# Sixteen transposed products of 512x512: two PSUM banks per copy, no block, transposes between halves, and a small early write

## The chip, the cores and the metric

The kernel runs on one core of one Trainium2 chip. The metric is the device time of one execution in microseconds; lower is better. A profiled execution also gives a span, from the first to the last instruction of the core.

## The reference

```python
def setup_inputs():
    batch, m, k, n = 16, 512, 512, 512
    return {
        "a": np.random.randn(batch, k, m).astype(np.float32),
        "b": np.random.randn(batch, n, k).astype(np.float32),
    }

def reference(a, b):
    return np.matmul(a.transpose(0, 2, 1), b.transpose(0, 2, 1)).astype(np.float32)
```

Both inputs come transposed. TensorE wants the contracted axis k on the partitions for both operands: a has it there already, b has n there and must be turned first. Each of a, b and the output is 1 MB (1.049 million bytes) per batch, so an execution reads 33.55 MB and writes 16.78 MB.

## The kernel before

Each batch i goes through the same steps, spread over five engines that meet at semaphores. All waits are written out by hand inside one critical section (L42), and the engines' programs stand in a `Block` (L99): each engine branches into its own part at the start, and at the end of the block all engines meet at a barrier before the critical section ends with one of its own.

- SyncE issues all DMAs on one queue: the load of b (L108), the load of a (L111) and, five batches later (`LAG`), the store of a finished batch (L123). Each moves 128 rows of 8 KB. There are four input buffers for each of a and b (`LOADS`) and seven output buffers (`OUTS`). The load of b waits until the transposes of the batch four earlier are done (semaphore `turned`), the load of a until the first group of matmuls of that batch is done (`summed`). A store waits for `summed` to reach a later batch, which shows that the copies are over; the last two stores wait for the copies' own semaphores (L122).
- VectorE casts b to bfloat16 (`cast`, L145). TensorE transposes it as pairs of bfloat16 that are taken for one float32: eight transposes per batch (`transposes`, L78) into `bt_ps`. VectorE copies the result to SBUF (`turn`, L151).
- ScalarE casts a to bfloat16 (L183).
- TensorE does the product in four groups of four matmuls (`matmuls`, L90). Group rm fills one PSUM bank, `o_ps[rm]`, and counts up `summed`.
- VectorE copies the groups 0 and 2 out of PSUM (L167), ScalarE 1 and 3 (L194), one bank per copy. Each copy gives its bank back by a semaphore (`od_go` or `oa_go`), which TensorE takes before it fills the bank again.
- GpSimd builds the identity matrix for the transposes (L129, L131).

TensorE's order is: transposes of batch i+1, product of batch i, and so on; a loop of two batches per turn is followed by a tail:

```python
multiply(0, 0, steady)
turn(1)
pe.wait_ge(ac2_go, 1)
multiply(1, 1, last)
```

In this tail batch 14 is multiplied, batch 15 transposed and multiplied. There the cast of a is shared between ScalarE (first half) and VectorE (second half, L175, semaphore `ac2_go`).

Of the kernel before, what the change touches and what calls it, by code (L numbers as in the profile page):

```python
# [11 lines left out]
def kernel(  # L12
# [6 lines left out]
    nc = tc.nc  # L19
    P = 128  # L20
    B, K, M = a.shape
    _, N, _ = b.shape
    KO = K // P
    KJ = KO // 2
    MO = M // P
    NO = N // P
    assert B % 2 == 0

    f32 = mybir.dt.float32
    cdt = mybir.dt.bfloat16  # L30
# [3 lines left out]
    a_v = a.rearrange("b (ki ko) m -> b ki ko m", ko=KO)  # L34
    b_v = b.rearrange("b (ni no) k -> b ni no k", no=NO)
    out_v = out.rearrange("b (mi mo) n -> b mi mo n", mo=MO)

    LOADS = 4
    OUTS = 7
    LAG = 5  # L40

    with tc.tile_critical():  # L42
        sb = lambda name, shape, dt: ctx.enter_context(nc.sbuf_tensor(name, shape, dt))
        ps = lambda name, shape, dt: ctx.enter_context(nc.psum_tensor(name, shape, dt))
        sem = tc.alloc_semaphore
        a_sb = [sb(f"a_sb{s}", [P, KO, M], f32) for s in range(LOADS)]
        b_sb = [sb(f"b_sb{s}", [P, NO, K], f32) for s in range(LOADS)]
        o_sb = [sb(f"o_sb{s}", [P, MO, N], f32) for s in range(OUTS)]
        a_bf = [sb(f"a_bf{s}", [P, KO, M], cdt) for s in range(2)]
# [1 line left out]
        bt_sb = [sb(f"bt_sb{s}", [P, KJ, N], f32) for s in range(2)]  # L51
        identity = sb("identity", [P, P], f32)
        bt_ps = [ps(f"bt_ps{s}", [P, KJ, NO, P], f32) for s in range(2)]
        o_ps = [ps(f"o_ps{s}", [P, N], f32) for s in range(MO)]


        a_in = [sem(f"a_in{s}") for s in range(LOADS)]
# [2 lines left out]
        turned = sem("turned")  # L60
# [4 lines left out]
        bt_go = sem("bt_go")  # L65
        ac_go = sem("ac_go")
        ac2_go = sem("ac2_go")
        oa_go = sem("oa_go")
        od_go = sem("od_go")

        def transposes(pe, x, y):

            w = b_bf[x][:].bitcast(f32).rearrange("p no (pk j) -> p no j pk", j=KJ)
            for j in range(KJ):
                for no in range(NO):
                    last = pe.transpose(bt_ps[y][:, j, no, :], w[:, no, j, :], identity[:])  # L78
            last.then_inc(turned, 1)

        def take(pe, s):
            pe.wait_ge(s, 1).then_inc(s, -1)  # L82

        def matmuls(pe, x, y, waits):
            a_r = a_bf[x][:].rearrange("p rk (pm rm) -> p rk rm pm", rm=MO)
            bt_h = bt_sb[y][:].bitcast(cdt).rearrange("p j (n h) -> p j h n", h=2)
            for rm in range(MO):
                waits(rm)
                for rk in range(KO):
                    last = pe.matmul(  # L90
                        o_ps[rm][:],
                        a_r[:, rk, rm, :],
                        bt_h[:, rk // 2, rk % 2, :],
                        start=(rk == 0),
                        stop=(rk == KO - 1),
                    )
                last.then_inc(summed, 1)

        with nc.Block() as block:  # L99

            @block.sync
            def _(sp):
                for i in range(B + LAG):
                    s, use = i % LOADS, i // LOADS
                    if i < B:
                        if use:
                            sp.wait_ge(turned, i - LOADS + 1)
                        sp.dma_start(b_sb[s][:], b_v[i]).then_inc(b_in[s], 16)  # L108
                        if use:
                            sp.wait_ge(summed, MO * (i - LOADS) + 1)  # L110
                        sp.dma_start(a_sb[s][:], a_v[i]).then_inc(a_in[s], 16)  # L111
                    j = i - LAG
                    if j >= 0:


                        if j + 2 < B:
                            sp.wait_ge(summed, MO * (j + 2))
                        else:

                            sp.wait_ge(summed, MO * (B - 1))  # L120
                            for s in (oa_go, od_go):
                                sp.wait_ge(s, 2 * (j + 3 - B))  # L122
                        sp.dma_start(out_v[j], o_sb[j % OUTS][:]).then_inc(o_out[j % OUTS], 16)  # L123
                for s in range(OUTS):
                    sp.wait_ge(o_out[s], 16 * len(range(s, B, OUTS)))

            @block.gpsimd
            def _(pool):
                pool.memset(identity[:], 0.0).then_inc(id_go, 1)  # L129
                pool.wait_ge(id_go, 1)  # L130
                pool.affine_select(  # L131
                    out=identity[:],
                    in_=identity[:],
                    compare_op=mybir.AluOpType.not_equal,
                    fill=1.0,
                    base=0,
                    pattern=[[-1, P]],
                    channel_multiplier=1,
                ).then_inc(id_go, 1)

            @block.vector
            def _(dve):
                def cast(i):
                    dve.wait_ge(b_in[i % LOADS], 16 * (i // LOADS + 1))
                    dve.tensor_copy(b_bf[i % 2][:], b_sb[i % LOADS][:]).then_inc(bc_go, 1)  # L145

                def turn(i):


                    dve.wait_ge(turned, i + 1)  # L150
                    dve.tensor_copy(  # L151
                        bt_sb[i % 2][:].rearrange("p j (ni no) -> p j ni no", no=NO),
                        bt_ps[i % 2][:].rearrange("p j no ni -> p j ni no"),
                    ).then_inc(bt_go, 1)

                dve.sem_inc(od_go, 2)
                cast(0)
                cast(1)
                turn(0)
                for i in range(B):  # L160
                    if i + 2 < B:
                        turn(i + 1)
                    if i >= OUTS:
                        dve.wait_ge(o_out[i % OUTS], 16 * (i // OUTS))
                    for rm in (0, 2):
                        dve.wait_ge(summed, MO * i + rm + 1)
                        dve.tensor_copy(o_sb[i % OUTS][:, rm, :], o_ps[rm][:]).then_inc(od_go, 1)  # L167
                        if rm == 0 and i + 2 < B:
                            cast(i + 2)
                    if i + 2 == B:  # L170
                        turn(i + 1)

                        s = (i + 1) % LOADS
                        dve.wait_ge(a_in[s], 16 * ((i + 1) // LOADS + 1))
                        dve.tensor_copy(  # L175
                            a_bf[(i + 1) % 2][:, KO // 2:, :], a_sb[s][:, KO // 2:, :]
                        ).then_inc(ac2_go, 1)

            @block.scalar
            def _(act):  # L180
                def cast(i, part=slice(None)):
                    act.wait_ge(a_in[i % LOADS], 16 * (i // LOADS + 1))
                    act.copy(a_bf[i % 2][:, part, :], a_sb[i % LOADS][:, part, :]).then_inc(ac_go, 1)  # L183

                act.sem_inc(oa_go, 2)
                cast(0)
                for i in range(B):
                    if i + 2 < B:
                        cast(i + 1)
                    if i >= OUTS:  # L190
                        act.wait_ge(o_out[i % OUTS], 16 * (i // OUTS))
                    for rm in (1, 3):
                        act.wait_ge(summed, MO * i + rm + 1)
                        act.copy(o_sb[i % OUTS][:, rm, :], o_ps[rm][:]).then_inc(oa_go, 1)  # L194
                    if i + 2 == B:
                        cast(i + 1, slice(0, KO // 2))

            @block.tensor
            def _(pe):
                def steady(rm):  # L200
                    take(pe, (od_go, oa_go)[rm % 2])

                def last(rm):
                    pe.wait_ge((od_go, oa_go)[rm % 2], 1 + rm // 2)

                def multiply(x, y, waits):
                    take(pe, bt_go)
                    take(pe, ac_go)
                    matmuls(pe, x, y, waits)

                def turn(x):
                    take(pe, bc_go)
                    transposes(pe, x, x)

                pe.wait_ge(id_go, 2)
                turn(0)
                with pe.Fori(0, B // 2 - 1) as _i:
                    turn(1)
                    multiply(0, 0, steady)
                    turn(0)  # L220
                    multiply(1, 1, steady)
                multiply(0, 0, steady)
                turn(1)
                pe.wait_ge(ac2_go, 1)
                multiply(1, 1, last)


# [28 lines left out]
```

## Time and profile before

| What | Value |
|---|---|
| Median of 5 runs | 127.44 us (127.03 to 127.9) |
| Profiled execution | 127.25 us |
| its span | 125.1 us |
| mean granted TensorE clock in it | 0.899 |
| TensorE busy, share of the span | 88.6 us, 71% |
| VectorE busy | 59.4 us, 47% |
| ScalarE busy | 49.1 us, 39% |
| DMA queue of SyncE, share of 16 engines | 96.3% |

The page has these views: the busy time of each engine, the span in slices, the DMA queues, the chain of waits that ended last, and groups of instructions with what released them. Further views are answers to questions: an engine's instructions in order of time with their start and duration, all instructions of one source line, and stretches of the span. A row of the stretches has the stretch, its length, busy time and count of instructions for TensorE matmul (PE), weight load (PEld), VectorE (DVE), ScalarE (ACT) and GpSimd (POOL), then the granted clock, the busy share of the 16 DMA engines and the GB/s that they moved. A share can come out slightly over 1 in a short stretch, since a packet's whole time is counted where it starts.

### The profile page before, as it was taken

To read this page: it belongs to the slowest core of one execution; us is meant where nothing else is said; L and a number is where in the kernel's file an instruction comes from. 1 tells how busy PE (TensorE), PEld (TensorE's weight loads), DVE (VectorE), ACT (ScalarE), POOL (GpSimd) and SP (SyncE) were. 2 spreads that over 40 slices of the span, in tenths; PEclk is the share of its full clock that TensorE was granted. 3 is DMA by queue.
4 is the path that set the end of the run, shared out by engine and by line. 5 is a ranking of instruction groups with operands and counts; after the bars stand their busy time and mean duration, and the time that the engine had idled before them with its cause. 6 is when DMAs were issued, how large, how long until landed. Compare 5 with 4: busy or idle time off the path is not lost. (4 is left out here: it accounts for less than half of the span.)

```text
span 125.1 us, 1151 instructions
## 1 busy us (share of the span) xinstructions
PE 88.6 (71%) x384; PEld 49.0 (39%) x384; DVE 59.4 (47%) x65; ACT 49.1 (39%) x49; POOL 0.7 (1%) x6
## 2 busy tenths in 40 slices
PE   0061999999994929549694699928969199949800
PEld 0051636646643406243361535505344165433200
DVE  0125566796655537056560565526265544762200
ACT  4032617467561716314362233714326162340300
POOL 2000000000000000000000000000000000000000
PEclk9999999999999999985999558997699959996875
DMA  2999999999999999999999999999999999999981
GB/s 73 424 424 427 427 427 422 424 419 419 403 422 422 424 416 430 419 422 427 427 432 419 424 414 427 427 422 424 424 424 430 427 422 422 424 430 437 393 330 47
DMA packets 6914, 50.35 MB, mean 402 GB/s; under 512 B 768, under 2 KB 768, under 8 KB 768
## 3 DMA queue, kind: packets, MB, share of 16 engines
q1 hardware_dynamic: 6912, 50.33, 96.3%
q14 instruction: 2, 0.02, 0.1%
HBM read 33.55 MB, written 16.78 MB: 402 GB/s over the span
## 5 line engine op out<-in xcount | busy, mean ns | idle before, releaser
L90 PE MATMUL o_ps<-bt_sb,a_bf 128*128 128x512 bf16 x256 | 70.0, 432 | 2.1 <-PEq L82 2.1
L90 PEld LDWEIGHTS o_ps<-bt_sb,a_bf 128*128 128x128 bf16 x256 | 30.8, 121 | 36.1 <-issue 15.3
L183 ACT CAST a_bf<-a_sb 128x2048 bf16<-128x2048 f32 (+1 forms) x16 | 29.6, 1848 | 30.7 <-DMA a_sb<-in_a_dram 30.7
L78 PE MATMUL bt_ps<-identity,b_bf 128*128 128x128 f32 x128 | 22.0, 325 | 27.5 <-PEq L82 27.5
L145 DVE CAST b_bf<-b_sb 128x2048 bf16<-128x2048 f32 x16 | 19.6, 1225 | 35.0 <-DMA b_sb<-in_b_dram 35.0
L194 ACT COPY o_sb<-o_ps 128x512 f32<-128x512 f32 x32 | 18.8, 586 | 38.1 <-PE o_ps L90 37.8
L78 PEld LDWEIGHTS bt_ps<-identity,b_bf 128*128 128x128 f32 x128 | 19.2, 212 | 32.7 <-issue 31.9
L151 DVE COPY bt_sb<-bt_ps 128x1024 f32<-128x1024 f32 x16 | 19.6, 1225 | 15.3 <-PE bt_ps L78 15.3
L167 DVE COPY o_sb<-o_ps 128x512 f32<-128x512 f32 x32 | 21.8, 685 | 8.4 <-PE o_ps L90 8.4
L183 ACT ACT_TABLE_LOAD x1 | 1.3, 1283 | 1.0 <-SPq L42 1.0
L175 DVE CAST a_bf<-a_sb 128x1024 bf16<-128x1024 f32 x1 | 0.7, 683 | 0.0
L131 POOL TENSOR_SCALAR_AFFINE_SELECT identity<-identity 128x128 f32<-128x128 f32 x1 | 0.3, 292 | 0.2 <-POOL identity L129 0.2
L129 POOL MEMSET identity<- 128x128 f32 x1 | 0.2, 204 | 0.5 <-SPq L42 0.5
L240 POOL MEMSET const-bfloat16-1.0<- 128x1 bf16 x1 | 0.1, 101 | 0.0
L240 POOL MEMSET const-uint8-127<- 128x1 uint8 x1 | 0.1, 101 | 0.0
L240 POOL MEMSET const-float32-0.0<- 128x1 f32 x1 | 0.1, 98 | 0.2 <-issue 0.2
L240 POOL MEMSET const-float32-1.0<- 128x1 f32 x1 | 0.1, 98 | 0.0
## 6 DMA issues: line engine op xcount, KB each, us to landing
b_sb<-in_b_dram SPq DMA_DIRECT2D x16, 1024.0 KB, 18.1
a_sb<-in_a_dram SPq DMA_DIRECT2D x16, 1024.0 KB, 19.2
out_dram<-o_sb SPq DMA_DIRECT2D x16, 1024.0 KB, 17.9
```

The lines of the kernel that those rows point to most:

```text
L78: last = pe.transpose(bt_ps[y][:, j, no, :], w[:, no, j, :], identity[:])
L90: last = pe.matmul(o_ps[rm][:], a_r[:, rk, rm, :], bt_h[:, rk // 2, rk % 2, :], start=(rk == 0), stop=(rk == KO - 1),)
L129: pool.memset(identity[:], 0.0).then_inc(id_go, 1)
L131: pool.affine_select(out=identity[:], in_=identity[:], compare_op=mybir.AluOpType.not_equal, fill=1.0, base=0, pattern=[[-1, P]], channel_ ...
L145: dve.tensor_copy(b_bf[i % 2][:], b_sb[i % LOADS][:]).then_inc(bc_go, 1)
L151: dve.tensor_copy(bt_sb[i % 2][:].rearrange("p j (ni no) -> p j ni no", no=NO), bt_ps[i % 2][:].rearrange("p j no ni -> p j ni no"),).then ...
L167: dve.tensor_copy(o_sb[i % OUTS][:, rm, :], o_ps[rm][:]).then_inc(od_go, 1)
L175: dve.tensor_copy(a_bf[(i + 1) % 2][:, KO // 2:, :], a_sb[s][:, KO // 2:, :]).then_inc(ac2_go, 1)
L183: act.copy(a_bf[i % 2][:, part, :], a_sb[i % LOADS][:, part, :]).then_inc(ac_go, 1)
L194: act.copy(o_sb[i % OUTS][:, rm, :], o_ps[rm][:]).then_inc(oa_go, 1)
L240: nc = _bacc.Bacc("TRN2", target_bir_lowering=False, num_devices=1)
```

## The change

It has four parts.

1. **Two banks per copy.** The four one-bank tiles become two of two banks. VectorE copies groups 0 and 1 in one instruction, ScalarE groups 2 and 3. TensorE takes one semaphore for each half of the product (`half`) in place of one per group. For the last batch the copies stay one bank each: VectorE 0 and 2, ScalarE 1 and 3. The stores' wait for `summed` goes from 4(j+2) to 4(j+1)+3.
2. **No block.** The same programs are functions called one after another, so there are no branches into a block and no barrier at its end. The critical section's own barrier stays.
3. **Transposes of the last batch between the halves.** In TensorE's tail the transposes of batch 15 move from behind the product of batch 14 to between its halves. VectorE copies batch 14's first half before it turns batch 15; ScalarE casts its half of the last a before it copies batch 14's second half.
4. **An early write.** ScalarE, once the identity exists, issues a DMA that writes its first 16 columns (64 bytes per partition) to the place of the first batch's output. The store of batch 0 waits for it (`first`) and overwrites it.

```diff
-        o_ps = [ps(f"o_ps{s}", [P, N], f32) for s in range(MO)]
+        o_ps = [ps(f"o_ps{s}", [P, MO // 2, N], f32) for s in range(2)]
...
-        with nc.Block() as block:
-            @block.sync
-            def _(sp):
...
-                        if j + 2 < B:
-                            sp.wait_ge(summed, MO * (j + 2))
-                        else:
-                            sp.wait_ge(summed, MO * (B - 1))
-                            for s in (oa_go, od_go):
-                                sp.wait_ge(s, 2 * (j + 3 - B))
-                        sp.dma_start(out_v[j], o_sb[j % OUTS][:]).then_inc(o_out[j % OUTS], 16)
...
+        def run_sp(sp):
...
+            def store(j):
+                if j + 2 < B:
+                    sp.wait_ge(summed, MO * (j + 1) + 3)
+                else:
+                    sp.wait_ge(summed, MO * (B - 1))
+                    sp.wait_ge(od_go, 1 if j + 2 == B else 3)
+                    sp.wait_ge(oa_go, 1 if j + 2 == B else 3)
+                if j == 0:
+                    sp.wait_ge(first, 16)
+                sp.dma_start(out_v[j], o_sb[j % OUTS][:]).then_inc(o_out[j % OUTS], 16)
...
+        def copy_out(eng, i, rm):
+            s = i % OUTS
+            q = rm if isinstance(rm, int) else rm.stop - 1
+            if s != i:
+                eng.wait_ge(o_out[s], 16 * (i // OUTS))
+            eng.wait_ge(summed, MO * i + q + 1)
+            copy = eng.copy if eng is nc.scalar else eng.tensor_copy
+            h = q // 2
+            p = rm - 2 * h if isinstance(rm, int) else slice(None)
+            go = oa_go if eng is nc.scalar else od_go
+            copy(o_sb[s][:, rm, :], o_ps[h][:, p, :]).then_inc(go, 1)
...
+        def run_dve(dve):
...
+            dve.sem_inc(od_go, 1)
+            cast(0)
+            cast(1)
+            turn(0)
+            for i in range(B - 2):
+                turn(i + 1)
+                copy_out(dve, i, slice(0, 2))
+                cast(i + 2)
+            copy_out(dve, B - 2, slice(0, 2))
+            turn(B - 1)
+            cast_a(dve, B - 1, slice(KO // 2, KO)).then_inc(ac2_go, 1)
+            copy_out(dve, B - 1, 0)
+            copy_out(dve, B - 1, 2)
+
+        def run_act(act):
+            act.sem_inc(oa_go, 1)
+            act.wait_ge(id_go, 2)
+            act.dma_start(out_v[0][:, 0, :16], identity[:, :16]).then_inc(first, 16)
+            cast_a(act, 0, slice(None)).then_inc(ac_go, 1)
+            for i in range(B - 2):
+                cast_a(act, i + 1, slice(None)).then_inc(ac_go, 1)
+                copy_out(act, i, slice(2, 4))
+            cast_a(act, B - 1, slice(0, KO // 2)).then_inc(ac_go, 1)
+            copy_out(act, B - 2, slice(2, 4))
+            copy_out(act, B - 1, 1)
+            copy_out(act, B - 1, 3)
...
+            def half(x, h, wait):
...
+                wait((od_go, oa_go)[h])
+                for q in range(2):
+                    for rk in range(KO):
+                        last = pe.matmul(
+                            o_ps[h][:, q, :],
...
+                        )
+                    last.then_inc(summed, 1)
...
-                multiply(0, 0, steady)
-                turn(1)
-                pe.wait_ge(ac2_go, 1)
-                multiply(1, 1, last)
+            take(bt_go)
+            take(ac_go)
+            half(0, 0, take)
+            turn(1)
+            half(0, 1, take)
+            pe.wait_ge(ac2_go, 1)
+            take(bt_go)
+            take(ac_go)
+            half(1, 0, lambda s: pe.wait_ge(s, 1))
+            half(1, 1, lambda s: pe.wait_ge(s, 1))
```

## The prediction

> **What bounds the kernel now.** I read the page first: the shares of the engines, the DMA rows, and then the chain that ended last. They disagree at first sight.
>
> ```profile
> PE 88.6 (71%) x384; PEld 49.0 (39%) x384; DVE 59.4 (47%) x65; ACT 49.1 (39%) x49; POOL 0.7 (1%) x6
> ...
> q1 hardware_dynamic: 6912, 50.33, 96.3%
> ...
> PE o_ps L90 4%; ACT o_sb L194 0%
> ```
>
> No compute engine is busy throughout, and the one DMA queue in use is at 96.3% of 16 engines. The chain (last line) covers only 4%: it begins at 112.82 us with the sixteen matmuls of the last batch. So I cut the span into stretches, with the DMA share and GB/s at the right of each row.
>
> ```profile
> 0.00:2.60 2.60, 0.00 (x0) 0.00 (x0) 0.00 (x0) 1.28 (x1) 0.70 (x6) 1.00 0.16 19
> 2.60:31.00 28.40, 20.89 (x95) 12.93 (x96) 15.70 (x17) 12.54 (x11) 0.00 (x0) 1.00 1.01 423
> 31.00:33.00 2.00, 2.00 (x11) 0.97 (x10) 2.00 (x3) 0.77 (x2) 0.00 (x0) 1.00 0.93 360
> 33.00:118.00 85.00, 65.48 (x282) 35.11 (x280) 41.59 (x47) 33.91 (x35) 0.00 (x0) 0.88 1.01 425
> 118.00:121.00 3.00, 0.25 (x2) 0.00 (x0) 0.08 (x1) 0.58 (x1) 0.00 (x0) 0.90 0.74 306
> ```
>
> From 2.6 to 118 us the DMA engines run without a pause at 423 to 425 GB/s. One megabyte takes 1.0486 MB / 0.424 = 2.47 us, so the 48 transfers alone are 118.7 us. Only four places are left for a gain: the 2.6 us before the queue is full, a dip at 31 to 33, a hole at 118 to 121, and what follows the last byte. The dip loses (424 - 360) / 424 x 2 = 0.30 us, and falls where the first store begins: twelve loads stand ahead of it, 2.6 + 12 x 2.47 = 32.2. The hole loses (424 - 306) / 424 x 3 = 0.83 us. Its reason is the next pair: SyncE issues the last store only at 118.94, after ScalarE's last copy (118.29 + 0.58); the one before it waited for nothing so late.
>
> ```profile
> 112.86 5.40 PE o_ps L90 x16
> ...
> 118.94 0.33 SPq L123 DMA_DIRECT2D out_dram<-o_sb  x1
> ```
>
> **The change, part by part.**
>
> *The block goes.* At the head SyncE passes the program's own barrier at 0.7 us, branches at 0.8 and issues its first load at 0.94. Without the branch it can issue at about 0.8: gain 0.15 us (0 to 0.2), all on the path, since everything behind it is one full queue. At the end the block's barrier stands between the last landing and the barrier of the critical section:
>
> ```profile
> L99 SPq COMPARE_BRANCH x1: 33/33/33, 123.5 to 123.5; - x1
> L99 SPq DRAIN x1: 7/7/7, 123.7 to 123.7; - x1
> L99 SPq EVENT_SEMAPHORE x1: 17/17/17, 123.8 to 123.8; - x1
> ...
> L42 ACTq DRAIN x1: 14/14/14, 123.9 to 123.9; - x1
> ```
>
> From 123.5 to just under 123.9 only this barrier runs, and nothing hides it. The barriers at L42 and L251 stay. Gain 0.35 us (0.3 to 0.4).
>
> *The last transposes between the halves.* Before: the product of batch 14 ends at 109.8 (ScalarE copies its last group at 109.83), then eight transposes take 1.11 us from 109.64, VectorE's turn 1.23 from 110.79 and its half cast 0.68 from 111.93; TensorE resumes at 112.86. After: batch 14's first half ends at 108.0 (ScalarE's copy of its second group starts at 108.06), and batch 15's b is cast by 107.0 (105.76 + 1.23), so the transposes run 108.0 to 109.2 and the second half 109.2 to about 110.9. VectorE copies the first half 108.0 to 109.3, turns to 110.5 and casts to 111.2. TensorE starts the last product at about 111.25, 1.6 us earlier. The new order puts VectorE's copy of batch 14 ahead of the turn, which is why it isn't 1.85. ScalarE casts its half of a before the copy of batch 14's second half; a lands near 108.2 (b15 was ready at 105.7, one transfer earlier), the cast takes 1.05, and the copy's data are ready only at 110.9: no delay. With the old 5.40 us the product ends at 116.65, the last copy at 117.25, the last store is issued at 117.35. In the trace its data start 0.85 us after the issue (118.94 to about 119.8), so now at 118.2.
>
> What that buys is less than 0.83. The sixteen DMA engines are not level. At 0.2 us a row the share is never zero in the hole:
>
> ```profile
> 119.40:119.60 0.20, 0.00 (x0) 0.00 (x0) 0.00 (x0) 0.00 (x0) 0.00 (x0) 1.00 0.19 82
> ...
> 122.40:122.60 0.20, 0.00 (x0) 0.00 (x0) 0.00 (x0) 0.00 (x0) 0.00 (x0) 0.50 0.10 41
> 122.60:122.80 0.20, 0.00 (x0) 0.00 (x0) 0.00 (x0) 0.00 (x0) 0.00 (x0) 0.50 0.10 41
> ```
>
> Some three engines are still on the store before when the last one is issued. The trace's packet records show store 14 finished between 118.41 and 120.09, engine by engine, and store 15 at 122.3 to 122.4 on fourteen, 122.54 on one, and 123.09 on one with a single 0.67 us packet where 0.31 is usual. The fast engines gain up to 1.4 us, but the kernel waits for all: the engine at 120.09 needs eight more packets of 0.31, 122.5. So the gain is 0.5 in this execution (123.09 to 122.55), about 0 where no late engine meets a long packet, 0.8 if the engines level out. I take 0.35. It needs the store in time for the first engine, 118.4; up to about 1 us of lateness costs only part of it.
>
> Here the Trainium skill's "TensorE: Matmul & The Clock Gate", "Part 1", bears. The granted clock is 0.50 from 114 to 116 us and the product takes 5.40 us, where sixteen matmuls at full clock take 109.8 - 106.2 = 3.6. The page says the gate halves the clock after an idle window of about 3.4 us and needs about as long a busy one to open. With a gap of 0.35 in place of 2.12 the rule would give 3.6, the store issued at 115.5; by the row it is 117.35. Both are before 118.4, so the sum is the same.
>
> *Two banks per copy.* VectorE's two copies of 685 ns per batch become one of 1024 elements; the nearest row is the turn, L151, 1024 elements out of PSUM at 1225 ns. ScalarE's two of 586 become one of about 1.05 (its 1024-element cast). Each saves some 0.13 us a batch, and TensorE waits twice instead of four times. TensorE now gets a bank back only when two are copied. All this is worth nothing: the cover is the queue, where a transfer lands 18 us after issue against 2.47 of service, seven deep. If that cover went, batch time would be set by TensorE, 88.6 / 16 = 5.5 us against 7.4. The stores' wait on SyncE is one group of four matmuls looser, so the loads queued behind it are issued 0.9 to 1.7 us earlier: also nothing. Stores 12 to 14 of the end come later by the inserted transposes (store 14: 112 instead of 110.5, waiting for ScalarE's wide copy), but the fast engines need 14 only near 116.
>
> *The early write.* ScalarE waits for the identity (1.67 us), issues a DMA of 128 pieces of 64 bytes, then goes on; its first cast waits for data until 8.19, so 0.4 us of issue and the 1.28 of the table load are hidden. Store 0 waits for the write, which has over 20 us. The pieces reach the engines near 2.6, just as the loads fill them, so their service is on the path. Nearest row: every transfer ends in 16 small packets (768 under 512 B in all), and the loads still move 423 GB/s. By that row eight pieces per engine cost under 0.1. Against it stands the skill's "DMA: Bandwidth & Descriptors": "Specifications" has writes under 512 B done as read-modify-write, and "Measured" puts small packets at about 10.5 ns each, so 128 would be an estimated 1.3 us if one held up all sixteen engines. No row shows a write of that kind to HBM. I take 0.15 (0.05 to 1.3). What it can bring is the dip at the first store, 0 to 0.30; later stores begin without one so deep, so some of it belongs to the first write alone. I take 0.2. Net gain 0.05 (0.25 gain to 1.3 loss).
>
> *Sum:* 0.15 + 0.35 + 0.35 + 0.05 = 0.90. The profiled execution took 127.25, its span 125.1 and 2.15 around it, which I leave as it is (a second queue in use could add to it; bounded at 0 to 0.3). 127.25 - 0.9 = 126.35. The median of the runs is 127.44, 0.19 above, so I predict 126.5.
>
> **The rivals.**
> *Only the barrier counts.* The late engines set the end, the dip stays and the branch was hidden: 0.35 to 0.5, 127.0. For it: the spread of 1.7 us among engines. Against: the long packet seen in the tail. Chance 0.28.
> *Everything is collected.* Hole 0.8, dip 0.3, barrier and branch 0.5: 1.6, 125.8. Chance 0.15. Against it, the same spread.
> *The early write blocks the engines.* At 2.6 to 5 us, each engine meets its small writes between two loads and holds its queue until they are confirmed. The last store needed 4.5 us from issue to landing, 2.47 of it service: 2.0 for the rest. If the engines stand still that long the load queue loses 2.0, less 0.85 gained elsewhere: 128.6, slower. It is slower than the bound from a stall of 1.5 us on. Against it: store 0's start, also a write between loads, lost only 0.30. Chance 0.07.
> *The last product isn't earlier*, because VectorE's wide copy delays the turn or SyncE's store waits elsewhere: 126.9, inside the first rival.
>
> **How the numbers follow.** About 0.5% (0.64 us) is what a measurement of this kernel can tell from no change: the line is 126.8. My forecast has 0.50, nearly all beyond it; with the 0.15 of the full gain and a few hundredths lost to noise, faster is 0.63. The first rival gives same 0.29, the last faults slower 0.08. The range 125.7 to 127.3 holds full gain and barrier-only, and leaves out the blocking write.
>
> **What would show it.** Right: no L99 barrier in the end part and about 0.35 us less from the last landing to the end; the first load issued near 0.8; the last product starting near 111.2; the last store issued before 118; the share in 118 to 121 near 1; the dip near 32 smaller. Wrong: a dip before 5 us larger than 0.3; the last landing still 123.3 or later after a store issued in time; VectorE's wide copy above 1.4 us.

## The result and the profile after

The changed kernel's median is 126.70 us (126.35 to 127.23, 42 runs), that of the kernel before, measured beside it, 127.07 us (126.39 to 128.21, 79 runs). The ratio is 0.9966, 95% interval 0.9954 to 0.9977: 0.43 us faster, give or take 0.15. That is half of the 0.90 us that the prediction summed up. The time lies inside the forecast range; by the forecast's own line of 0.5% it is the case "same", to which it gave 0.29, and not "faster", to which it gave 0.63.

The page of the changed kernel, the same rows as before. The chain now ends with the last product at another line, because the code moved; the queue q10 is the early write.

```profile
PE 83.1 (67%) x384; PEld 46.7 (38%) x384; DVE 58.9 (47%) x50; ACT 46.7 (38%) x34; POOL 0.7 (1%) x6
...
q1 hardware_dynamic: 6912, 50.33, 97.0%
q10 hardware_dynamic: 144, 0.01, 0.1%
...
PE o_ps L201 3%; ACT o_sb L136 0%; ACTq L131 0%
```

The stretches of the span, with the DMA share and GB/s at the right:

```profile
0.00:2.60 2.60, 0.00 (x0) 0.00 (x0) 0.00 (x0) 0.45 (x1) 0.70 (x6) 1.00 0.21 32
2.60:31.00 28.40, 18.51 (x82) 11.05 (x83) 14.34 (x12) 11.24 (x9) 0.00 (x0) 1.00 1.01 420
31.00:33.00 2.00, 2.00 (x14) 1.41 (x13) 1.07 (x1) 1.82 (x2) 0.00 (x0) 1.00 0.96 315
33.00:118.00 85.00, 62.63 (x292) 34.20 (x289) 43.53 (x38) 33.20 (x25) 0.00 (x0) 0.96 1.01 426
118.00:121.00 3.00, 0.00 (x0) 0.00 (x0) 0.00 (x0) 0.00 (x0) 0.00 (x0) 0.61 1.00 423
121.00:123.00 2.00, 0.00 (x0) 0.00 (x0) 0.00 (x0) 0.00 (x0) 0.00 (x0) 0.50 0.27 115
```

The hole at 118 to 121 is not there (423 GB/s where it was 306). The dip at the first store is not smaller but deeper (315 against 360). The head is as it was. In order of time, the end of the compute work and the last store:

```profile
107.06 1.19 PE L192 MATMUL bt_ps<-identity,b_bf 128*128 128x128 f32 x8 [0.73 <-PEq L182]
108.09 1.98 PE L201 MATMUL o_ps<-bt_sb,a_bf 128*128 128x512 bf16 x8
...
110.36 3.81 PE L201 MATMUL o_ps<-bt_sb,a_bf 128*128 128x512 bf16 x16 [0.30 <-PEq L182]
...
114.93 0.33 SPq L96 DMA_DIRECT2D out_dram<-o_sb  x1
```

The transposes stand between the halves of batch 14, TensorE waits 0.30 us before the last product instead of 2.12, the product takes 3.81 instead of 5.40 us, and the last store is issued 4.0 us earlier. Yet the span is only 0.9 us shorter in these two executions, and less in the mean of many. The first load shows why part of it is missing. Below it stand SyncE's early branch before the change and after:

```profile
0.94 0.38 SPq L79 DMA_DIRECT2D b_sb<-in_b_dram  x1
```

```profile
L251 SPq COMPARE_BRANCH  x1: 33/33/33, 0.8 to 0.8; - x1
...
L266 SPq COMPARE_BRANCH  x1: 33/33/33, 0.8 to 0.8; - x1
```

The branch at 0.8 us belongs to the program's outer lines (L251 before, L266 after), not to the block at L99, and the first load leaves at 0.94 as before. The end of the program (line L42, the critical section's barrier) shows another part:

```profile
L42 ACTq DRAIN x1: 8/8/8, 123.0 to 123.0; - x1
```

The last landing is at 122.77 and the span ends at 124.23: 1.46 us, where it was 123.45 to 125.11, 1.65.

### The profile page after: what moved, and what is told of

It is laid out like the page before. It is cut to its first block, busy times and chain, and to the rows that moved or that the text cites. A ratio compares the mean times of both kernels' runs of the same rounds, so it can differ in the third digit from the quotient of the medians.

```text
span 124.2 us, 1084 instructions
## 1 busy us (share of the span) xinstructions
PE 83.1 (67%) x384; PEld 46.7 (38%) x384; DVE 58.9 (47%) x50; ACT 46.7 (38%) x34; POOL 0.7 (1%) x6
## 5 line engine op out<-in xcount | busy, mean ns | idle before, releaser
L201 PE MATMUL o_ps<-bt_sb,a_bf 128*128 128x512 bf16 x256 | 64.3, 405 | 0.3 <-PEq L182 0.3
L192 PE MATMUL bt_ps<-identity,b_bf 128*128 128x128 f32 x128 | 21.4, 317 | 30.7 <-PEq L182 30.7
L201 PEld LDWEIGHTS o_ps<-bt_sb,a_bf 128*128 128x128 bf16 x256 | 29.7, 116 | 29.4 <-issue 5.6
L192 PEld LDWEIGHTS bt_ps<-identity,b_bf 128*128 128x128 f32 x128 | 18.2, 211 | 37.6 <-issue 37.6
L136 ACT COPY o_sb<-o_ps 128x1024 f32<-128x1024 f32 (+1 forms) x17 | 16.4, 963 | 39.4 <-PE o_ps L201 39.4
L136 DVE COPY o_sb<-o_ps 128x1024 f32<-128x1024 f32 (+1 forms) x17 | 19.7, 1162 | 15.0 <-PE o_ps L201 15.0
```

Of the source, the lines that this page charges most:

```text
L136: copy(o_sb[s][:, rm, :], o_ps[h][:, p, :]).then_inc(go, 1)
L192: last = pe.transpose(bt_ps[x][:, j, no, :], w[:, no, j, :], identity[:])
L201: last = pe.matmul(o_ps[h][:, q, :], a_r[:, rk, 2 * h + q, :], bt_h[:, rk // 2, rk % 2, :], start=(rk == 0), stop=(rk == KO - 1),)
```

## The experiments

My theory after the result: the hole was worth little, because the slowest DMA engines had nearly no pause in it; the block cost 0.2 us; the early write costs a little and brings nothing. The rivals: the early write pays by warming the stores, or the hole pays in full, or the block is the whole gain. Twelve experiments followed, nine new kernels and three repeats, each with 12 timed runs beside 33 or 35 of the kernel before on the same chip.

| Kernel | Ratio to before (95%) | Mean span less before's | Outside the span |
|---|---|---|---|
| changed, again | 0.9958 (0.9937 to 0.9978) | -0.56 | 2.15 |
| changed, no early write | 0.9955 (0.9933 to 0.9977) | -0.52 | 2.19 |
| the same, again | 0.9962 (0.9938 to 0.9987) | -0.39 | 2.12 |
| changed, block back | 0.9983 (0.9963 to 1.0004) | -0.13 | 2.09 |
| changed, old transposes | 0.9969 (0.9950 to 0.9988) | -0.51 | 2.28 |
| changed, last store 3 us late | 0.9968 (0.9943 to 0.9993) | -0.44 | 2.20 |
| changed, last store 5 us late | 0.9987 (0.9962 to 1.0012) | -0.27 | 2.20 |
| before and the early write | 0.9993 (0.9973 to 1.0014) | -0.10 | 2.15 |
| before without the block | 1.0015 (0.9988 to 1.0042) | -0.43 | 2.65 |
| the same, again | 1.0025 (0.9995 to 1.0054) | -0.19 | 2.64 |
| changed, block back, no write | 1.0008 (0.9979 to 1.0037) | -0.17 | 2.26 |
| changed, no write, stores in pairs | 0.9990 (0.9961 to 1.0019) | -0.13 | 2.14 |

The last two columns are worked out from each run's device time and span, in us: the mean span less that of the kernel before on the same chip (good to about 0.2), and the mean of time less span (good to 0.1; up to 0.2 where it is 2.65). Before's own part outside the span is 2.16, 2.17 and 2.18 on the three chips. The first run without the early write, the block put back, the old transposes, and before with the write share one chip; the changed kernel again, the second run without the write and the two late stores a second; the last four rows a third. The changed kernel itself did not run on the third, so these four rows may differ from the others by the chip as well. No version was shown to beat the changed kernel.

**The early write, taken away.**

```diff
-            act.wait_ge(id_go, 2)
-            act.dma_start(out_v[0][:, 0, :16], identity[:, :16]).then_inc(first, 16)
...
-                if j == 0:
-                    sp.wait_ge(first, 16)
```

> The changed kernel without the early write and without the wait for it; everything else as changed. Theory 1 (the early write only costs: about 0.1 us of small packets, a slower ramp, and it does not shrink the dip at the first store): 0.1 to 0.3 us faster than the changed kernel, so about 0.5 to 0.7 us under the kernel before; GB/s over 2.6 to 31 us back from 420 to about 423. Theory 2 (the early write warms the stores, the slow packets at later stores in the profile of before come back without it): 0.2 to 0.4 us slower than the changed kernel, so level with before.

0.9955. The second time, beside the changed kernel itself:

> The changed kernel without the early write, a second time beside the changed kernel itself. If the early write costs its 144 small packets (9 per engine at 11 ns, 0.1 us) and brings nothing: 0.1 us faster, inside the interval. If it warms the first store: slower by 0.2 or more.

0.9962, against 0.9958 for the changed kernel run there:

> The changed kernel as it is, on the same chip as its three neighbours: 0.9966 of the kernel before within 0.002.

**The early write alone**, added to the kernel before with the same two pieces:

> The kernel before with only the early write added (and the wait of the first store for it). Theory 1 (it only costs): 0.1 to 0.3 us slower than before, the dip at 31 to 33 us not smaller than the 0.30 us of before. Theory 2 (it warms the stores): 0.2 to 0.4 us faster, dip gone or slow packets at the later stores gone.

0.9993. In none of these pairs does the write move the time beyond the interval, so what it is worth lies between about -0.3 and +0.3 us. The profiles narrow it. Two rows of 31 to 33 us, the first of the changed kernel without the write on its first run, the second of the same kernel on its second:

```profile
31.00:33.00 2.00, 2.00 (x13) 1.48 (x14) 0.89 (x1) 2.00 (x2) 0.00 (x0) 1.00 0.96 283
```

```profile
31.00:33.00 2.00, 2.00 (x12) 1.11 (x11) 1.23 (x1) 1.30 (x1) 0.00 (x0) 1.00 1.05 406
```

One and the same kernel has the deepest dip and nearly none. Over all profiles with this order of stores, GB/s in these two microseconds is 347 in the mean of seven with the write (315 to 373) and 343 of six without (283 to 406). The write does not warm the first store. What it costs is small too: the packet records, which list the start and duration of every DMA packet, give 11 ns for each of its packets, eight and one of 9 ns per engine, 0.1 us; by 10 us the kernels with it have begun 378.3 packets of 8 KB in the mean (374 to 382), those without 382.3 (375 to 385), and 4 packets at 52 per us are 0.08 us. The later packets of over 0.4 us did not come back without it either (19 behind 36 us in the mean with the write, 21 without). The packets speak for theory 1, a cost of about 0.1 us; the times cannot tell it from nothing.

The write didn't come when I said. The rows of ScalarE's issue and of its time to landing:

```profile
1.71 0.41 ACTq L170 DMA_DIRECT2D out_dram<-identity  x1
```

```profile
out_dram<-identity ACTq DMA_DIRECT2D x1, 8.0 KB, 6.9
```

It landed 6.9 us after the issue: its packets moved between 5.6 and 8.2 us, one for each load packet of an engine, and not at 2.6.

**The block put back** around the changed kernel's five programs:

```diff
-        run_sp(nc.sync)
...
+        with nc.Block() as block:
+            @block.sync
+            def _(sp):
+                run_sp(sp)
...
```

> The changed kernel with its five programs put back into a block. Theory 1 (the block's barrier costs only its own drain and semaphores, since a branch stays at both ends): 0.2 us slower than the changed kernel, the last landing to the end of the span 1.65 us instead of 1.46. The forecast's step (0.35 at the end and 0.15 at the head): 0.5 us slower, which would leave nothing of the gain.

0.9983, on the same chip as the kernels without the block at 0.9955 (no write) and 0.9969 (old transposes): 0.2 to 0.4 us slower, with intervals that overlap. From the last landing to the end it takes 1.67 us against 1.46, as theory 1 has it. The last part is the same in all profiles, whatever else a kernel does: 1.65 to 1.67 with the block (4 profiles), 1.45 to 1.46 without it and with the two-bank copies (8). So 0.20 us is shown for the block's barrier in the changed kernel. The mean span says 0.38 (-0.13 beside -0.52 and -0.51), good to about 0.25; where more than the 0.20 would come from, no trace shows.

**The block taken from the kernel before**, nothing else, run twice:

```diff
-        with nc.Block() as block:
-            @block.sync
-            def _(sp):
+            def run_sp(sp):
...
+            run_sp(nc.sync)
...
```

> The kernel before with only its block taken away. Theory (a drain and one round of semaphores, 0.21 us, is all that the block costs): last landing to the end 1.45 us instead of 1.65, first load still issued at 0.94, 0.2 us faster, ratio 0.998. The forecast's step: 0.5 us faster, ratio 0.996. Rival (the block is worth the whole gain): ratio 0.9966.

> The kernel before without its block, a second time, for a narrower interval: ratio 0.998 by the theory, 0.996 by the forecast's step.

1.0015 and 1.0025: no gain at all. All three expectations of a gain fell. The table tells where it went: the spans are shorter, by 0.43 and 0.19, but the part outside the span is 2.65 and 2.64 where it is 2.18 in the kernel before. Two rows of the end show something new. The first is of before without the block, ScalarE's drains in the program's last barriers (shortest, median and longest ns, then first and last start); the second is the same of the changed kernel.

```profile
L252 ACTq DRAIN  x2: 8/74/139, 123.9 to 124.3; - x2
```

```profile
L266 ACTq DRAIN  x2: 8/8/8, 123.1 to 123.7; - x2
```

ScalarE comes 0.28 us later than the other engines to this barrier (its drain starts at 123.91, TensorE's and VectorE's at 123.64) and its drain takes 139 ns instead of 8; the second run has the same, 138 ns. From the last landing to the end it is 1.60 us, so that only 0.05 of the 0.20 is left. The instruction queue, q14, also fetches a piece of code near there, from 124.60, half a microsecond after that drain has ended, so this fetch did not hold the drain. The DMA rows of before without the block from 124 to 124.9 us, and of the kernel before from 119.9 to 120.7:

```profile
q14 instruction: 1, 0.01, 3.3%
```

```profile
q1 hardware_dynamic: 33, 0.26, 77.8%
q14 instruction: 1, 0.01, 5.2%
```

With the one-bank copies there are two fetches of code in the second half of the run: near 98 us, and at 118.6 to 120.0 with the block or 124.6 to 124.7 without it, when the kernel's work is over. With the two-bank copies (VectorE has 50 operations instead of 65, ScalarE 34 instead of 49) there is one, at 117.4 to 118.6, block or not, and the part outside the span is 2.09 to 2.28. So the removal of the block paid only together with the wide copies.

The packet records run on behind the span and show where the time outside it lies. In every profile one more fetch of code, 16 KB on queue q8, begins 1.0 to 1.8 us behind the end of the span and takes 0.93 to 1.40 us. In 13 of the 14 profiles the time outside the span is the end of this fetch, counted from the end of the span, less 0.21 to 0.25 us (less 0.12 in the other one, the block put back), so it moves with this fetch. In both profiles of before without the block the fetch begins 1.83 us behind the span, in before 1.21. That the late q14 fetch is what delays it is my reading and isn't shown: no run moved a fetch by itself, and in the changed kernel with the store late by two the q8 fetch begins 1.71 us behind the span although its q14 fetch came at 117.9.

**The transposes put back** behind the product of batch 14:

```diff
-            turn(1)
             half(0, 1, take)
+            turn(1)
```

> The changed kernel with TensorE's transposes of batch 15 back behind the whole product of batch 14. Theory 1 (the hole at 118 to 121 was worth 0.3 us, because late DMA engines fill part of it): last store issued 1 to 2 us later, 0.2 to 0.4 us slower than the changed kernel. Theory 2 (the late engines set the end alone): same time within 0.1 although the hole is back. Full value of the hole: 0.8 us slower.

0.9969, mean span 0.51 below before's: as fast as the changed kernel. The pause before the last product is back (2.11 us), but the last store still leaves early enough, and the row at 118 to 121 has 412 GB/s:

```profile
111.68 3.79 PE L201 MATMUL o_ps<-bt_sb,a_bf 128*128 128x512 bf16 x16 [2.11 <-PEq L182]
...
116.23 0.33 SPq L96 DMA_DIRECT2D out_dram<-o_sb  x1
```

So the time is that of theory 2, but the hole did not come back, and this run doesn't test what a hole costs. Beside the first profile of the changed kernel the moved transposes bring the store forward by 1.3 us; beside its second profile, whose last store leaves at 116.14, by 0.1.

The hole was missing even before the transposes moved. Three more profiles keep the old copies and the old order: before with the early write (store at 118.12) and both of before without the block (117.68 and 117.73). They have 423, 423 and 426 GB/s at 118 to 121. The last product of before with the write, and the store and the row of before without the block:

```profile
113.64 3.80 PE L91 MATMUL o_ps<-bt_sb,a_bf 128*128 128x512 bf16 x16 [2.12 <-PEq L83]
```

```profile
117.68 0.33 SPq L122 DMA_DIRECT2D out_dram<-o_sb  x1
...
118.00:121.00 3.00, 0.00 (x0) 0.00 (x0) 0.00 (x0) 0.00 (x0) 0.00 (x0) 0.68 1.01 423
```

What sets the profile of before apart is the clock: 0.50 from 114 to 116 us and 5.40 us for the last product, where the other three, with the same pause of 2.1 us in front, have 1.00 and 3.80 or 3.81. At 3.80 the product would have ended 1.6 us earlier and the last store's data started at about 118.2 (an estimate from 119.8), ahead of 118.41, where the first engine was done with the store before. So its hole comes from this slow product.

**The last store made late**, by two and by three casts on ScalarE into unused memory between the last batch's copies:

```diff
             copy_out(act, B - 1, 1)
+            for d in range(2):
+                act.copy(idle[d][:], a_sb[0][:])
             copy_out(act, B - 1, 3)
```

> The changed kernel with two extra casts of 128x2048 (1.9 us each) on ScalarE between the last batch's two copies, into unused memory: the last store is issued 2.5 to 3 us later, near 117.7, about where the kernel before issues it on a good run. Theory 1 (the hole was filled by late DMA engines, so that the earlier last store bought only what is beyond about 118): within 0.15 us of the changed kernel. Rival (each 0.1 us of lateness after the fast engines are done counts in full): also near nothing, since 117.7 plus 0.85 is close to 118.4; both then part in the next run.

> The same with three extra casts: last store issued near 119.6, its data from about 120.4, that is 2 us after the first engine is done with the store before. Theory 1 (the slowest engine sets the end and is busy until about 120): 0.3 to 0.8 us slower than the changed kernel. Rival (full value): 2.0 us slower. If the hole is worth nothing at all up to there: the same.

0.9968 and 0.9987. With two casts the store leaves at 117.81 and the time is that of the changed kernel within its interval, as theory 1 has it. With three it leaves at 120.21 and the hole is back, deeper than in the kernel before:

```profile
118.00:121.00 3.00, 0.00 (x0) 0.00 (x0) 0.00 (x0) 2.13 (x2) 0.00 (x0) 0.81 0.53 224
```

Its mean span is 0.29 us above the changed kernel's on that chip and its time 0.37, which is at the edge of what these intervals can tell; the 2.0 us of the rival is excluded. The packet records tell where the end comes from. Each of the sixteen DMA engines closes its share of a transfer with one small packet, which gives, for the last store, when the first and the last engine were done:

| Last store issued | First engine done | Last engine done |
|---|---|---|
| 114.93 (changed) | 120.92 | 122.40 |
| 115.50 (no write) | 120.94 | 123.01 |
| 116.23 (old transposes) | 120.90 | 122.85 |
| 117.81 (late by two) | 121.16 | 123.04 |
| 118.12 (before and write) | 121.47 | 123.26 |
| 118.94 (before) | 122.29 | 123.09 |
| 120.21 (late by three) | 123.55 | 123.75 |

Up to 118 the last engine is done between 122.4 and 123.04 however early the store was issued: that engine is late by itself, by 1.5 to 2.1 us against the first. A store pays only for what it ends beyond that. In the kernel before, at 118.94, fourteen engines end level and were done by 122.42, still no later than the late engine elsewhere. At 120.21 all end together, and the last at 123.75, 0.8 above the mean of the six others; this profiled execution was a long one, 0.56 us over its kernel's mean span.

**Both compute edits alone** (the changed kernel with the block back and without the write):

> The changed kernel with the block back and without the early write, so that only the two-bank copies and the moved transposes remain. Theory (what remains closes the hole at the end, and late DMA engines leave 0.2 us of its 0.8): 0.1 to 0.35 us faster than before, last store issued before 117, all engines done by 122.4 to 123.1, last landing to the end 1.65. Rival (the hole is worth nothing): the same as before.

1.0008, with a mean span 0.17 below before's and 2.26 outside. The last store is issued at 115.04, all engines are done by 122.55, and 1.65 us follow the last landing, as expected; the gain in time did not show. The span speaks for 0.2 us, the time for none, and the interval holds both: inconclusive. Why the part outside is 2.26 here and 2.09 in the kernel with the block and the write stays open; in the profiles the q8 fetch begins 1.54 us behind the span here and 0.99 there.

**The stores in pairs**, an attempt at making the late engines less late:

```diff
-                if i >= LAG:
-                    store(i - LAG)
+                j = i - LAG
+                if j >= 1 and j % 2:
+                    store(j - 1)
+                    store(j)
```

> The changed kernel without the early write, with the stores issued two at a time, every second batch. If the long packets of over 0.4 us that make some DMA engines late come from the change between loads and stores, half as many changes give fewer of them, the engines end closer together, and the time falls by 0.1 to 0.4 us against the changed kernel. If they don't, the same time within the interval; if the first store's delay leaves less behind the last load, slower by up to 0.5.

0.9990, no gain. The dip at 31 to 33 is gone (422 GB/s), and none stands where the first store now begins (422 at 37 to 39). But 22 packets of over 0.4 us remain behind 36 us, where the profiles of the other kernels have 10 to 31, and the engines end between 120.98 and 122.66. What makes some packets long isn't found, and neither is why this kernel shows no gain where the same one without pairs had 0.9955 and 0.9962 on other chips.

## Why the prediction was half right

That 126.70 came within 0.2 us of 126.5 is in part luck. The forecast took 0.94 off a kernel before of 127.44, the median of five runs; its median over 79 was 127.07, and the change took off 0.43. Of the signs that were to show it right, three came in both profiles of the changed kernel (no L99 barrier, the store before 118, a full share at 118 to 121), the start of the last product in one (110.36; 111.58 in the other, for 111.2), and three did not (0.35 less at the end, the first load at 0.8, a smaller dip).

- *What bounds the kernel:* right. The queue moves 422 to 427 GB/s from 33 to 118 us in every profile, and the only term that a trace locates, the block's barrier, stands behind its last byte.
- *The block, head, 0.15:* wrong, 0. The branch at 0.8 us is still in the program without the block, and the first load leaves at 0.94 or 0.95 in all profiles. I took the branch of the program (L251) for the block's.
- *The block, end, 0.35:* mis-sized, 0.20. I counted everything from 123.5 to 123.9, but a branch (L79, at 122.84) stays between the last landing and L42, and it takes the first 0.15 us; only the block's own drain and semaphores went. And the prediction left the part outside the span as it is: taking away the block alone adds 0.47 us there. With the wide copies, which I had costed at nothing, it does not.
- *The transposes:* the order came as forecast in the first profile (transposes at 107.06 to 108.25 for 108.0 to 109.2, last product at 110.36 for 111.25), but the value of 0.35 did not: the moved transposes alone are worth nothing measurable, and at most about 0.2 belongs to all that brings the last store forward. Two readings failed. The hole of 0.83 was taken for a property of the kernel, but it stands only in the profile whose last product ran at half clock. And "0.5 in this execution" was read from one engine at 123.09 with a long packet. That packet is the fetch of code in the row at 119.9 to 120.7 above; the two profiles of before without the block have no fetch ahead of their end and still end at 122.94 and 123.01. Nor were "some three" engines still on store 14 when the last store was issued at 118.94, but eight, which end it at 119.06 to 120.09. The first rival had this right: the late engines set the end.
- *The early write:* cost about 0.1 (I took 0.15), gain 0 (I took 0.2). The dip at the first store differs as much between two profiles of one kernel as between kernels; I had taken one profile's dip for a property. The Trainium skill's page "DMA: Bandwidth & Descriptors", section "Measured", gives about 10.5 ns per small packet for another kind of transfer; here each took 11 ns, on sixteen engines side by side and not one after another, so the estimate of 1.3 us did not come. No cost of a read-modify-write appears beyond these 11 ns.
- *The clock:* the last product takes 3.80 us at full clock (I took 3.6), and that made no difference to the sum, as said. But the shorter gap isn't shown to be what brought the full clock: four profiles with a gap of 2.11 or 2.12 us (before with the write, the old transposes, before without the block twice) have 1.00 and 3.79 to 3.81 too.
- *Two banks per copy:* worth nothing on the path, as said; ScalarE's copy took 1.02 and VectorE's 1.23 us, as the nearest rows had it. What I left out is how they bear on the block: only with them does its removal add nothing outside the span.

The terms that stand are 0.20 for the block with the wide copies, up to 0.2 for what brings the last store forward, less 0.1 for the write. That is 0.1 to 0.3 and reaches the interval's 0.28 to 0.58 only at its edge. The kernels that keep the block are not clear of the kernel before (0.9983, 0.9993 and 1.0008), so with the wide copies in place the block may be worth most of the gain; the traces locate 0.20 of it, and what makes up the rest stays open. One more candidate, tested by no run, is the clock: of the 103 executions of the kernel before that stand beside the experiments, the 28 with a mean granted clock of 0.915 or less have a mean span of 125.5 us, the other 75 of 125.1, and of 56 of the changed kernel only one is as low. If that were a cause, rarer low clocks would bring an estimated 0.1 us (28/103 of 0.35).

## What to carry to other kernels

Where a full DMA queue bounds a kernel, look at when each DMA engine is done, not at the mean share: a pause that the fast engines have is free as long as one late engine is still working. A single profile's dip, hole or long packet is no property of a kernel until a second profile of it has it too: the hole that this change was to close stood in one of the four profiles with the old copies and order. And compare the time with the span: an edit that shortens the span can give it back outside.

## What the runs showed of the hardware

- The sixteen DMA engines, with equal shares of every transfer, end 1.5 to 2.1 us apart after 118 us of work where the last store is issued by 118.12; with one issued at 120.21 they end 0.2 us apart.
- Small packets of a second queue wait for their turn: one 64-byte packet for each 8 KB packet of an engine, 0.31 us apart, and the first of them 3.9 us after the issue.
- Code is fetched late in the run, 8 KB on q14, and when it is fetched changed with the copies and the block: 118.6 to 120.0 or 124.6 to 124.7 with the one-bank copies, 117.4 to 118.6 with the two-bank ones.
- Behind the span a last fetch of 16 KB on q8 begins after 1.0 to 1.8 us, and the time outside the span moves with it: it is the end of this fetch less 0.21 to 0.25 us in 13 of 14 profiles.
- A pause of 2.1 us ahead of sixteen matmuls did not by itself lower their granted clock: it stayed at 1.00 in four profiles of five.
